# Queries, keys and gates of the first layer with channels on the partitions

## The chip, the cores and the metric

The kernel runs on one core of a Trainium2 chip. The metric is the device time of one execution in microseconds; several executions of a kernel are timed, and the median is compared. One further execution is recorded by the hardware profiler, and the profile shown here is that execution.

The engines are named as in the profile: PE is the matrix engine (PEld its weight loads), DVE the vector engine, ACT the scalar engine, POOL the GpSimd engine, SP the queue that issues most DMAs. Matrix results land in PSUM, which has eight banks of 512 fp32 numbers on each of 128 partitions; everything else that is on the core lies in SBUF.

## The reference, cut to what matters

A backbone of two layers over 1024 latent tokens and 256 context tokens of width 1024, in fp32. Layer 0 mixes by windowed attention with 16 query heads and 4 key heads of 64 channels, layer 1 by latent attention. What the change touches is the projection of layer 0:

```python
def project(h):
    n = h.shape[1]
    q, k, v, g = jnp.split(h @ w_in, [A_WIDTH, A_WIDTH + A_KV_WIDTH, A_WIDTH + 2 * A_KV_WIDTH], axis=-1)
    ...
qx, kx, vx, gx = project(hx)      # latent
qc, kc, vc, gc = project(hc)      # context
qx = apply_rope(qx, cos, sin)
kx = apply_rope(kx, cos, sin)

def apply_rope(u, cos, sin):
    r1, r2, c1, c2 = jnp.split(u, 4, axis=-1)
    rot = jnp.concatenate([-r2, r1, -c2, c1], axis=-1)
    return u * cos + rot * sin
```

`w_in` has 2560 columns: 1024 for queries, 256 keys, 256 values, 1024 gates. `h` is the normalized, scaled and shifted input (adaLN); scale, shift and the output gates come from products of a conditioning vector with the 1024 x 3072 matrix `ada_w` of each layer. Only latent tokens are rotated. In a head of 64 channels the rotation pairs channel i with i + 16 inside each half of 32.

## The kernel before

**Precision.** A product of fp32 matrices is made of three: each operand is split into a high part (`hi`, a rounded copy by ACT) and a low part (`lo`, the difference, by DVE or POOL) in `split`, L118 to L121, and `mm3`, L123 to L127, adds hi x hi, lo x hi and hi x lo in PSUM. So each step over 128 input channels is three matmuls, and 1024 input channels are 24.

**Staging.** SBUF is two large arenas, addressed in KB per partition: `R` for matmul operands, `F` for the rest. The input lies in five tiles `hT[p]` of 256 tokens, channels on the partitions (p = 0 is the context, 1 to 4 are latent, tile p at 16 p KB of `R`). The columns of `w_in` are taken in ten blocks of 256 in the order of `blocks`, L341: values first (block 0), queries (1 to 4), two of gates (5, 6), keys (7), two of gates (8, 9). `fetch` (L344) and `load_w` (L296) load a block's weights in four quarters through a ring of four staging buffers `stg` and split them, low parts on POOL, into one of two places `wst`, so that block n + 1 is fetched when block n begins.

**One block of projection.** For each block and each tile p, `proj_mm` (L373) issues 2 x 24 matmuls in two halves j. For values, queries and keys the input is the stationary operand and the weights move (256 columns): tokens come out on the partitions. For gates it is the other way round: channels come out on the partitions, 256 tokens move. Results go to one of six PSUM banks in turn (`pss`, L115). `proj_out` (L390) takes them out: gates through ACT's Silu to DRAM (`g0_d`); values by a split into `V`; queries and keys of latent tokens by `rope` (L304): DVE multiplies with the cosines (L307), makes the two rotated halves times the sines (L312, twice), POOL adds (L317); the context is copied by DVE (L411). Since attention wants channels on the partitions, `rest` (L416) then transposes each rotated 128 x 128 piece on PE (L421, four for a tile, into banks 6 and 7) and splits the result, into `kT` for keys, and for queries through a ring `qst` to DRAM (`q0_d`) by four DMAs. The loop at L693 calls `rest` of a tile after the matmuls of the next one.

**Beside it.** The loop also advances a generator `ada_vec` (L355) that forms the remaining adaLN products: DVE multiplies a row block of `ada_w` by a scalar and adds it up (L192, L194; called adaLN steps below), the sum is split (low part on POOL) and summed over partitions by four small PE products (L209, two for the last of layer 1, which take a bank of `pss` too). `wo_load` (L610) loads and splits the sixteen halves of the output weights of layer 0 into `Wo`, which lies over `hT`; two are advanced per tile near the end of the projections and what is left when the second attention unit begins. `UnitA` (L475) is one attention unit (128 query tokens, one key head): `prep_q` loads its queries back from `q0_d`, `score` makes scores (L517, L518, L524 to L527), and so on. Layer 1 follows.

**What sets the order.** The program is written for five in-order queues; a scheduler of the framework places each engine's instructions from the program's order and their data, and may move them against each other. Each queue then runs in order and waits on semaphores.

## Time and profile before

| | us |
|---|---|
| median of 3 runs | 1670.13 (1668.36 to 1673.35) |
| profiled execution | 1673.18, span 1671.0, mean granted clock 0.993 |
| projections of layer 0, blocks 1 to 9 | 95 to 386 |
| attention of layer 0 | 386 to 780 |
| layer 1 | 780 to 1671 |

The stages were read off the timeline: the first query block's matmuls begin at 95 us, the last gate's Silu starts at 385.9 us. A row of a group has line, engine, operation, out<-in and shapes, then busy time and mean ns of one, then the idle time of the engine before it and what ended that. A row of windows has the window, its length, and the busy time and count of PE, PEld, DVE, ACT and POOL, then the granted PE clock, the DMA share and GB/s. A row of waits has who waited for whom: us in total, times, longest. A row of the timeline has start and length in us, engine, line, shape and count. Matmuls are pipelined: a matmul's length overlaps the next one's, so the spacing of starts is what PE pays.

### The profile page before, as it was taken

The numbers are of one execution on the slowest core, as the hardware profiler recorded it, in microseconds if no ns is written. First come the engines' busy times: TensorE is split into PE (matmuls) and PEld (weight loads), VectorE is DVE, ScalarE is ACT, GpSimd is POOL, SyncE is SP. The second block draws the span as 40 slices with busy tenths as digits, with TensorE's granted clock in tenths as the row PEclk, the third lists the DMA queues.
The fourth block names the chain that finished last, engine by engine and source line by source line (L and its number), as shares of the span: only waits on it lengthen the run. The fifth ranks groups of instructions, "written<-read, shape, count | busy, mean of one in ns | idle before, by whom it ended". The sixth has DMA issues, their size and how long they took to land.

```text
span 1671.0 us, 27005 instructions
## 1 busy us (share of the span) xinstructions
PE 1613.4 (97%) x9688; PEld 1304.9 (78%) x9688; DVE 975.4 (58%) x2066; ACT 833.5 (50%) x1790; POOL 783.3 (47%) x784
## 2 busy tenths in 40 slices
...
GB/s 304 146 173 207 177 214 84 74 145 128 113 105 89 93 89 92 89 93 201 27 64 243 222 71 74 95 54 20 60 32 38 49 20 53 39 84 69 46 156 65
DMA packets 128070, 175.38 MB, mean 105 GB/s; under 512 B 11184, under 2 KB 75312, under 8 KB 127936
## 3 DMA queue, kind: packets, MB, share of 16 engines
...
HBM read 127.47 MB, written 46.15 MB: 104 GB/s over the span
## 4 chain that ended last, share of the span: by engine, by line
PE 76%; DVE 11%; ACT 5%; issue 4%; DMA 2%; POOL 1%; SPq 0%; DVEq 0%; ACTq 0%; POOLq 0%
PE PB L125 16%; PE PB L127 16%; PE PB L126 16%; PE PB L1125 9%; PE PB L1091 4%; PE PB L555 3%; PE PB L545 3%; DVE arena_r L121 2%; DVE arena_f L194 2%; PE PB L517 2%; DVE arena_f L524 2%; PE PB L518 2%; DVE arena_f L275 1%; ACT arena_f L1110 1%; ACT arena_f L527 1%
## 5 line engine op out<-in xcount | busy, mean ns | idle before, releaser
L125 PE MATMUL PB<-arena_r 128*128 128x256 f32 (+3 forms) x2104 | 691.1, 329 | 5.2 <-ACT arena_r L278 4.1
L126 PE MATMUL PB<-arena_r 128*128 128x256 f32 (+3 forms) x2104 | 681.6, 324 | 2.8 <-DVE arena_r L280 1.5
L127 PE MATMUL PB<-arena_r 128*128 128x256 f32 (+3 forms) x2104 | 678.9, 324 | 0.7 <-DVE arena_r L121 0.7
L125 PEld LDWEIGHTS PB<-arena_r 128*128 128x128 f32 (+1 forms) x2104 | 403.0, 192 | 68.8 <-issue 26.1
L127 PEld LDWEIGHTS PB<-arena_r 128*128 128x128 f32 (+1 forms) x2104 | 402.8, 192 | 31.0 <-DVE arena_r L121 1.3
L126 PEld LDWEIGHTS PB<-arena_r 128*128 128x128 f32 (+1 forms) x2104 | 403.9, 192 | 28.1 <-DVE arena_r L280 3.2
L1117 POOL TENSOR_TENSOR arena_f<-arena_f 128x512 f32<-128x512 f32 x252 | 326.2, 1295 | 76.0 <-ACT arena_f L1110 60.9
L121 DVE TENSOR_TENSOR arena_r<-PB,arena_r 128x512 fp32r<-128x512 f32 (+5 forms) x263 | 168.1, 646 | 143.1 <-ACT arena_r L120 141.4
L1110 ACT ACTIVATE arena_f<-PB 128x512 f32<-128x512 f32 x320 | 189.2, 598 | 124.8 <-PE PB L127 111.8
L1095 DVE TENSOR_REDUCE arena_f<-PB 128x1 f32<-128x1280 f32 x128 | 190.5, 1488 | 97.4 <-PE PB L1091 95.0
L121 POOL TENSOR_TENSOR arena_r<-arena_f,arena_r 128x512 fp32r<-128x512 f32 x98 | 139.1, 1438 | 182.2 <-ACT arena_r L120 140.1
L120 ACT CAST arena_r<-PB 128x512 fp32r<-128x512 f32 (+5 forms) x263 | 142.5, 550 | 91.2 <-PE PB L545 25.1
L524 DVE CUSTOM_DVE_ANT_0 arena_f<-PB,arena_f,small 128x256 f32<-128x256 f32 (+1 forms) x288 | 146.2, 523 | 29.4 <-PE PB L518 23.2
L1125 PE MATMUL PB<-arena_f 128*64 128x512 f32 x640 | 156.0, 599 | 0.0
L527 ACT ACTIVATE arena_f<-arena_f,small 128x640 f32<-128x640 f32 (+2 forms) x160 | 119.4, 747 | 31.1 <-DVE small L526 30.4
L555 PE MATMUL PB<-arena_r 128*128 128x512 f32 x336 | 123.8, 441 | 3.3 <-ACT arena_f L566 2.1
L120 ACT CAST arena_r<-arena_f 128x512 fp32r<-128x512 f32 (+1 forms) x138 | 82.7, 609 | 87.4 <-PE PB L126 18.9
L194 DVE SCALAR_TENSOR_TENSOR arena_f<-arena_f,small 128x512 f32<-128x512 f32 x126 | 108.2, 910 | 7.8 <-DMA arena_f<-ada_w 7.4
L545 PE MATMUL PB<-ident,arena_f 128*128 128x128 f32 x672 | 110.1, 274 | 1.0 <-ACT arena_f L527 0.9
L1125 PEld LDWEIGHTS PB<-arena_f 128*64 128x64 f32 x640 | 43.3, 136 | 80.5 <-issue 79.3
L1091 PE MATMUL PB<-arena_r 96*128 96x512 f32 (+1 forms) x384 | 100.1, 369 | 1.2 <-DVE arena_f L1095 1.0
L545 PEld LDWEIGHTS PB<-ident,arena_f 128*128 128x128 f32 x672 | 83.3, 140 | 19.3 <-ACT arena_f L527 4.6
...
## 6 DMA issues: line engine op xcount, KB each, us to landing
arena_f<-ada_w SPq DMA_DIRECT2D x82, 256.0 KB, 3.4
arena_r<-q_d SPq DMA_DIRECT2D x80, 256.0 KB, 4.0
arena_f<-a_w_in SPq DMA_DIRECT2D x40, 256.0 KB, 3.4
q_d<-arena_f SPq DMA_DIRECT2D x80, 128.0 KB, 2.4
g_d<-arena_f SPq DMA_DIRECT2D x36, 256.0 KB, 3.1
...
arena_r<-qn_d SPq DMA_DIRECT2D x32, 256.0 KB, 3.6
```

The source lines that it names most:

```text
L120: nc.scalar.copy(hi, src)
L121: (lo_eng or nc.vector).tensor_sub(lo, src, hi.bitcast(F32))
L125: nc.tensor.matmul(o, ah, bh, start=first, stop=False)
L126: nc.tensor.matmul(o, al, bh, start=False, stop=False)
L127: nc.tensor.matmul(o, ah, bl, start=False, stop=last)
L524: nc.vector.tensor_tensor_reduce(o, S, mk, 1.0, prev, ALU.add, ALU.max, mx)
L545: nc.tensor.transpose(pt[:, h, :], self.Ps[h][:, ci * 128 : ci * 128 + 128], ident)
L555: nc.tensor.matmul(self.pv, V[:, self.chunks[ci], self.g, :], PT[:, s], start=ci == 0 and s == 0, stop=ci == self.m - 1 and s == 1,)
L1095: nc.vector.reduce_max(self.mx[:, 96 + b : 97 + b], psm[:, 0:TOK], AX.X, negate=True)
L1110: nc.scalar.activation(E, S, AF.Exp)
L1117: eng.tensor_add(self.acc, self.acc, E)
L1125: nc.tensor.matmul(self.pv[p : p + 64], Vq[:, c, self.h % 4, :], self.E.pop(c), start=c < 2, stop=c >= NT - 2)
```

## The change

For blocks 1 to 9 the weights become the stationary operand everywhere, so queries, keys and gates come out with channels on the partitions and nothing is transposed. `proj_t` replaces the old `proj_out` for them. The latent tokens are taken in two groups `gp` = 1, 2 of 512 (two neighbouring tiles seen as one moving operand in two pieces of 256, `hw`) and, for each, two channel halves `c` of 128: 24 matmuls of 512 each. The context (`gp` = 0) keeps 256 moving, 2 x 24 matmuls. Values (block 0) stay as they were.

The rotation of a group: DVE multiplies the bank with the cosines, a DVE shuffle exchanges channels i and i + 16 within each 32 partitions out of PSUM, POOL multiplies the shuffled copy with the (signed) sines and adds. The tables are now 128 channels x 1024 tokens each. `rest` splits queries from SBUF and stores them with four DMAs; for keys DVE adds the rotated halves itself, 64 partitions at a time.

Moved with it: the tables' place takes one of the four staging buffers of `stg`; blocks 8 and 9 run over latent group 1, latent group 2 and the context last, so that the tiles of `hT` come free in another order, and with them the places of `Wo` and of the first two query buffers `qtb`; two output-weight halves are advanced in each of the last six calls that are not of group 1, and two each at attention units 1 and 2.

```diff
@@ -321,9 +321,9 @@
     wst = [80, 96]
     kT = r_at(112, 4, TOK)
     V = r_at(132, NT, 4, 128)
-    cosa = f_at(0, 8, 64)
-    sina = f_at(2, 8, 64)
-    stg = Ring(F, [4, 6, 8, 10], 512)
+    cosa = f_at(0, SEQ)
+    sina = f_at(10, SEQ)
+    stg = Ring(F, [4, 6, 8], 512)
     xr = Ring(F, [14, 18, 48], 1024)
     xtr = Ring(F, [22, 30], 2048)
     ev = Ring(F, [38, 40, 42, 44, 46], 512)
@@ -371,73 +371,101 @@
     ada_steps = ada_vec()
     def proj_mm(bi, p, j, o, ka, kb):
+
         h, W, js = hT[p], wt[bi], slice(j * 128, j * 128 + 128)
         for k in range(ka, kb):
-            hk = [h[:, s, k, :] for s in range(2)]
-            wk = [W[:, s, k, :] for s in range(2)]
-            if blocks[bi] >= 1536:
-                mm3(o, [w[:, js] for w in wk], hk, k == 0, k == 7)
-            else:
-                mm3(o, [x[:, js] for x in hk], wk, k == 0, k == 7)
+            mm3(o, [h[:, s, k, js] for s in range(2)], [W[:, s, k, :] for s in range(2)], k == 0, k == 7)
     def proj_a(bi, p):
-        ps = PB[:, 4, :] if (bi, p) == (9, 4) else pss()
+        ps = pss()
         os = [ps[:, j * 256 : j * 256 + 256] for j in range(2)]
         for j in range(2):
             proj_mm(bi, p, j, os[j], 0, 8)
-        return proj_out(bi, p, os, ps)
...
-    def proj_out(bi, p, os, ps=None):
...
+        proj_out(bi, p, os)
+
+    def proj_out(bi, p, os):
+        for j in range(2):
+            ti = 2 * p + j
+            split(V[:, ti, :, 0:64], V[:, ti, :, 64:128], shp(os[j], 4, 64))
+
+
+    hw = [None]
+    for p in (1, 3):
+        two = R[:, 16 * p * KB : 16 * (p + 2) * KB]
+        hw.append(two.rearrange("p (q s k n) -> p q s k n", q=2, s=2, k=8))
+    swap = [(i + 16) % 32 for i in range(32)]
+
+    def proj_t(bi, gp, c):
+        W, c0 = wt[bi], blocks[bi]
+        ps = PB[:, 4, :] if (bi, gp) == (9, 0) else pss()
+        for cc in (c,) if gp else range(2):
+            if gp:
+                o = shp(ps, 2, 256)
+            elif c0 < 1024:
+                o = shp(ps, 2, 2, 128)[:, :, cc, :]
+            else:
+                o = ps[:, cc * 256 : cc * 256 + 256]
+            for k in range(8):
+                if gp:
+                    m = [hw[gp][:, :, s, k, :] for s in range(2)]
+                elif c0 < 1024:
+                    m = [shp(hT[0][:, s, k, :], 2, 128) for s in range(2)]
+                else:
+                    m = [hT[0][:, s, k, :] for s in range(2)]
+                mm3(o, [W[:, s, k, cc * 128 : cc * 128 + 128] for s in range(2)], m, k == 0, k == 7)
+        t0 = 256 + 512 * (gp - 1) if gp else 0
         if c0 >= 1536:
             g = ev.next()
             nc.scalar.activation(g, ps, AF.Silu)
             ch = (c0 - 1536) // 128
...
+            if gp:
+                load(out=g0_d[ch + c, :, t0 : t0 + 512], in_=g)
+            else:
+                load(out=g0_d[ch : ch + 2, :, 0:256].rearrange("c p n -> p c n"), in_=shp(g, 2, 256))
             return None
...
+        if gp == 0:
+            if c0 == 1024:
+                u = shp(ps, 2, 256)
+                for e in range(2):
+                    kh = kT[:, e::2, 0:256]
+                    split(kh[0:64], kh[64:128], u[64 * e : 64 * e + 64])
             else:
...
+                q = shp(qst.next(), 2, 512)
+                split(q[:, 0].bitcast(F32R), q[:, 1].bitcast(F32R), ps)
                 for e in range(2):
                     for s in range(2):
                         load(
...
+                            out=q0_d[c0 // 256, :, s, 0:2, e * 256 : e * 256 + 256],
+                            in_=shp(q[64 * e : 64 * e + 64, s], 2, 256),
                         )
...
+            return None
+        x0 = t0 - 256
+        a, r = ev.next(), ev.next()
+        nc.vector.tensor_mul(a, ps, cosa[:, x0 : x0 + 512])
+        nc.vector.stream_shuffle(out=r, in_=ps, mask=swap)
+        nc.gpsimd.tensor_mul(r, r, sina[:, x0 : x0 + 512])
+        if c0 < 1024:
+            nc.gpsimd.tensor_add(a, a, r)
+
+        def rest():
+            q = shp(qst.next(), 2, 512)
+            if c0 == 1024:
+                for e in range(2):
+                    es = slice(64 * e, 64 * e + 64)
+                    nc.vector.tensor_add(q[0:64, e], a[es], r[es])
+                    kh = kT[:, 2 * c + e, t0 : t0 + 512]
+                    split(kh[0:64], kh[64:128], q[0:64, e])
+                return
+            split(q[:, 0].bitcast(F32R), q[:, 1].bitcast(F32R), a)
+            for e in range(2):
+                for s in range(2):
+                    o0 = e * 256 + c * 128
+                    load(
+                        out=q0_d[c0 // 256, :, s, t0 // 128 : t0 // 128 + 4, o0 : o0 + 128],
+                        in_=shp(q[64 * e : 64 * e + 64, s], 4, 128),
+                    )
+
+        return rest
     mask = f_at(0, 384)
@@ -451,9 +479,9 @@
     Pr = Ring(F, [14 + 2.5 * i for i in range(8)], 640)
     gr = Ring(F, [1.5, 2.5, 46], 256)
     xr0 = Ring(F, [4], 1024)
-    Wo = [r_at(o, 2, 1024) for o in (0, 8, 16, 24, 32, 40, 48, 56)]
+    Wo = [r_at(o, 2, 1024) for o in (16, 24, 32, 40, 48, 56, 0, 8)]
     ogr = Ring(R, [64, 72], 2048)
-    qtb = [r_at(o, 2, 4, 128) for o in (56, 60, 80, 84, 108)]
+    qtb = [r_at(o, 2, 4, 128) for o in (72, 76, 80, 84, 108)]
     ptr = Ring(R, [88, 92, 96, 100, 104], 1024)
     pss3 = Banks(0, 1, 2)
     pst3 = Banks(6, 7, 3)
@@ -623,8 +651,8 @@
                 yield
 
     wo_fill = wo_load()
-    order = [(0, p) for p in range(2, NP)] + [(bi, p) for bi in range(1, 8) for p in range(NP)]
-    order += [(8, 0), (8, 1), (9, 0), (9, 1), (8, 2), (9, 2), (8, 3), (9, 3), (8, 4), (9, 4)]
+    order = [(bi, gp, c) for bi in range(1, 8) for gp in range(3) for c in range(2 if gp else 1)]
+    order += [(bi, gp, c) for gp in (1, 2, 0) for bi in (8, 9) for c in range(2 if gp else 1)]
     rest = None
     N1, N2 = 3, 7
 
@@ -690,36 +718,39 @@
     xts = {2: shp(xtr.next(), 8, 256)}
     turn_x(nx[4], xts[2], 0)
     turn_x(norm_x(src0(5), xr_0, junk), xts[2], 1)
-    for i, (bi, p) in enumerate(order):
-        if p == (3 if bi == 0 else 0) and bi + 1 < 10:
-            if bi == 0:
-                load(out=cosa, in_=t["cos_a"].rearrange("p (t d) -> p t d", t=8))
-                load(out=sina, in_=t["sin_a"].rearrange("p (t d) -> p t d", t=8))
+    for p in range(2, NP):
+        if p + 1 < NP:
+            xts[p + 1] = build_x(p + 1, src0, xr, xtr, junk)
+        build_h(p, xts.pop(p), hT[p], ada0.A, ada0.B)
+        if p == 3:
+            fetch(1)
+        proj_a(0, p)
+    load(out=cosa, in_=t["cos_a"])
+    load(out=sina, in_=t["sin_a"])
+    started = {0, 1}
+    for bi, gp, c in order:
+        if bi + 1 < 10 and bi + 1 not in started:
+            started.add(bi + 1)
             fetch(bi + 1)
-        if bi == 0:
-            if p + 1 < NP:
-                xts[p + 1] = build_x(p + 1, src0, xr, xtr, junk)
-            build_h(p, xts.pop(p), hT[p], ada0.A, ada0.B, fast=p == 0)
-        else:
-            steps(ada_steps, N1 if bi < 5 else N2 if bi < 7 else 100)
-        if (bi, p) == (9, 2):
+        steps(ada_steps, N1 if bi < 5 else N2 if bi < 7 else 100)
+        if (bi, gp, c) == (9, 2, 0):
             load2(out=mask, in_=t["mask"])
             load2(out=gx, in_=gate_d[0, 0, :].partition_broadcast(128))
             load2(out=gc, in_=gate_d[0, 1, :].partition_broadcast(128))
-        if (bi, p) == (8, 4):
+        if (bi, gp) == (8, 0):
             units[0].prep_q()
             units[0].prep()
             units[1].prep_q()
-        if (bi, p) == (9, 4):
+        if (bi, gp) == (9, 0):
             units[1].prep()
             units[2].prep_q()
             for h in range(4):
                 units[0].score(h)
-        r = proj_a(bi, p)
+        r = proj_t(bi, gp, c)
         if rest:
             rest()
         rest = r
-        if i > 40:
+        if bi >= 8 and gp != 1:
             for _ in range(2):
                 next(wo_fill, None)
 
@@ -738,9 +769,9 @@
     og = None
     fins = []
     for ui, u in enumerate(units):
-        if ui == 1:
-            for _ in wo_fill:
-                pass
+        if ui in (1, 2):
+            next(wo_fill, None)
+            next(wo_fill, None)
         if u.g == 0:
             og = shp(ogr.next(), 2, 8, 128)
             steps = 4 * u.m - 2
@@ -1415,8 +1446,8 @@
         "b_kv_norm": g("b_kv_norm")[0],
         "b_w_ukv": ukv,
         "b_w_out": g("b_w_out")[0],
-        "cos_a": tab(cos_a),
-        "sin_a": tab(sin_a),
+        "cos_a": np.tile(cos_a.T, (2, 1)),
+        "sin_a": np.tile(sin_a.T, (2, 1)),
         "cos_b": tab(cos_b),
         "sin_b": tab(sin_b),
         "mask": mask,
```

37 lines of the change are left out of this document (removed).

## The prediction

> **What bounds the kernel now.** I read four views: the page's head, the windows of the first layer's projection stage, who PE waited for there, and the timelines of PE, DVE and POOL in it. "L" numbers are the kernel's before.
>
> ```profile
> span 1671.0 us, 27005 instructions
> PE 1613.4 (97%) x9688; PEld 1304.9 (78%) x9688; DVE 975.4 (58%) x2066; ACT 833.5 (50%) x1790; POOL 783.3 (47%) x784
> ```
>
> ```profile
> core 0: us, PE busy (x) PEld busy (x) DVE busy (x) ACT busy (x) POOL busy (x), PEclk, DMA share, GB/s
> 95.00:130.00 35.00, 31.30 (x245) 30.36 (x243) 35.00 (x57) 7.69 (x13) 16.59 (x15) 0.95 0.70 199
> 130.00:165.00 35.00, 31.36 (x246) 30.49 (x245) 34.31 (x62) 6.39 (x11) 15.06 (x15) 0.95 0.71 209
> 165.00:201.00 36.00, 34.66 (x286) 33.70 (x284) 27.37 (x51) 6.38 (x11) 16.97 (x15) 1.00 0.65 179
> 201.00:230.00 29.00, 27.30 (x225) 26.35 (x224) 17.61 (x48) 6.09 (x11) 9.20 (x11) 1.00 0.60 162
> ```
>
> ```profile
> PE PB L421 <- POOL arena_f L317: 8.7, 8, 3.4
> PE PB L421 <- DVE arena_f L411: 1.7, 1, 1.7
> ```
>
> The four windows are query blocks 1 to 4. PE is the bound of the kernel. In blocks 1 and 2 it is not: DVE is full (35.00 of 35, 34.31 of 35), the granted clock is 0.95, and a block takes 35 us, while block 4, with less for DVE, takes 29. The link is the transposes, L421: PE's queue holds them behind the next group of matmuls, and they wait for the rotation of the group before (10.4 us in 90 to 386 us). So PE can run one group ahead of DVE and no more.
>
> **PE's own work.** Start times, to the hundredth:
>
> ```profile
> 215.48 0.28 PE L127 MATMUL PB<-arena_r 128*128 128x256 f32 x1
> 215.60 0.60 PE L421 MATMUL PB<-ident,arena_f 128*128 128x128 f32 x4
> 215.96 0.36 PE L125 MATMUL PB<-arena_r 128*128 128x256 f32 x1
> 216.16 0.28 PE L126 MATMUL PB<-arena_r 128*128 128x256 f32 x1
> 216.28 0.29 PE L127 MATMUL PB<-arena_r 128*128 128x256 f32 x1
> ...
> 889.98 0.39 PE L127 MATMUL PB<-arena_r 128*128 128x512 f32 x1
> 890.21 0.39 PE L125 MATMUL PB<-arena_r 128*128 128x512 f32 x1
> ...
> 891.34 0.39 PE L127 MATMUL PB<-arena_r 128*128 128x512 f32 x1
> ```
>
> ```profile
> L209 PE MATMUL PB<-arena_r 128*2 128x512 f32 x28 | 7.7, 403 | 0.0
> L517 PE MATMUL PB<-arena_r 128*128 128x256 f32 x12 | 3.7, 317 | 0.0
> ```
>
> A 256-wide matmul starts 0.12 us after the last (216.16, 216.28). A 512-wide one takes 0.227: from 889.98 to 891.34 are six steps, 1.36 us. Four transposes cost 0.44: without them the matmuls of 215.96 and 216.16 would stand at 215.60 and 215.72.
>
> - Blocks 1 to 9 issue 9 x 240 = 2160 matmuls of 256. After: 9 x 48 = 432 of 256 (context) and 9 x 96 = 864 of 512 (latent). Each of the 864 replaces two: 0.240 - 0.227 = 0.013, so -11.2 us.
> - The 100 transposes, 25 groups of four, go: 25 x 0.44 = -11.0 us.
> - From 95 to 386 us, 291 us, PE's work is 2160 x 0.12 + 11.0 = 270, the adaLN products (L209, 28 of 512 wide, 6.4), the first attention scores (L517 and as many L518, 24 of 256, 2.9) and small transposes (about 1): 280.5. The other 10.5 us are waits and the clock's dips, as the 10.4 above says. With the transposes gone, PE waits for nothing but free banks and weights: up to -10.5.
>
> Most that can be had: 11.2 + 11.0 + 10.5 = 33 us. The rule of back-to-back matmuls in the Trainium skill (TensorE: Matmul & The Clock Gate, section Back-to-back issue gap: N over 2.4, plus 2.5 ns, warm) speaks against the first term: 109 ns for 256 and 216 for 512, so 2.6 ns a pair, an estimate of 2.2 us in place of 11.2. Rows of this kernel have 120 and 227, and the sum goes by them.
>
> **DVE and POOL, which take the work over.** Rows from 84 to 229 us (last rotation of block 4), DVE busy 124.30 us; then rows for the new operations:
>
> ```profile
> 84.00:229.00 145.00, 134.62 (x1079) 131.08 (x1079) 124.30 (x222) 29.05 (x52) 64.68 (x57) 0.98 0.64 182
> ...
> L194 DVE SCALAR_TENSOR_TENSOR arena_f<-arena_f,small 128x512 f32<-128x512 f32 x84 | 77.6, 981 | 4.2 <-DMA arena_f<-ada_w 4.2
> L312 DVE TENSOR_TENSOR arena_f<-PB,arena_f 128x128 f32<-128x128 f32 x62 | 14.8, 280 | 0.0
> L307 DVE TENSOR_TENSOR arena_f<-PB,arena_f 128x256 f32<-128x256 f32 x32 | 13.3, 415 | 15.0 <-PE PB L127 15.0
> L121 DVE TENSOR_TENSOR arena_f<-PB,arena_f 128x512 fp32r<-128x512 f32 x18 | 12.2, 680 | 0.0
> L411 DVE COPY arena_f<-PB 128x256 f32<-128x256 f32 x8 | 3.0, 410 | 0.0
> ...
> L121 POOL TENSOR_TENSOR arena_r<-arena_f,arena_r 128x512 fp32r<-128x512 f32 x26 | 41.3, 1613 | 13.1 <-ACT arena_r L120 6.5 <-PE PB L126 3.7 <-PE PB L127 2.9
> L317 POOL TENSOR_TENSOR arena_f<-arena_f 128x256 f32<-128x256 f32 x30 | 22.4, 750 | 67.0 <-DVE arena_f L312 51.2 <-PE PB L209 13.6 <-PE PB L126 2.1
> ```
>
> ```profile
> L121 DVE TENSOR_TENSOR arena_r<-arena_f,arena_r 128x512 fp32r<-128x512 f32 x32 | 28.8, 910 | 44.6 <-ACT arena_r L120 29.2 <-PE PB L126 15.4
> L604 POOL TENSOR_TENSOR arena_f<-arena_f 128x512 f32<-128x512 f32 x18 | 23.2, 1288 | 58.6 <-DVE arena_f L603 35.1 <-DVE small L526 19.7 <-DVE small L538 3.8
> L120 ACT CAST arena_r<-arena_f 128x512 fp32r<-128x512 f32 x130 | 79.5, 620 | 84.6 <-PE PB L126 18.9 <-DMA arena_f<-a_w_out 13.3 <-PE PB L127 12.3
> ```
>
> Per latent group of a query block (16 of them), after: one product with the cosines out of PSUM (0.68, as the 680 row), one shuffle, one subtraction of the high part, now SBUF from SBUF (0.91). No row has a shuffle. It reads 128x512 f32 out of PSUM and writes SBUF as the 680 row does, and has one operand less: I take 0.68; the ends are the 0.41 of half its size and 1.49, the dearest DVE read of PSUM here (1280 wide). The Trainium skill (VectorE: DVE Perf Modes, section The perf-mode tier table) gives about 2400 ns for 2048 elements; a quarter is an estimate of 0.6, which would change DVE's sum by 1.3 us and the path by nothing.
>
> ```profile
> L1095 DVE TENSOR_REDUCE arena_f<-PB 128x1 f32<-128x1280 f32 x128 | 190.5, 1488 | 97.4 <-PE PB L1091 95.0
> ```
>
> - Removed from DVE: 14.8 + 13.3 + 12.2 + 3.0 = 43.3 us. Added: 16 x (0.68 + 0.68 + 0.91) + 4 x 0.68 (context) = 39.0.
> - POOL: 32 adds of 0.75 become 32 operations (a product with the sines, an add) of 1.29: 24 becomes 41 us, POOL 64.7 becomes 82 of 145. Not a bound. But POOL's long operations hold DVE's adaLN steps up:
>
> ```profile
> 88.46 8.88 DVE L194 SCALAR_TENSOR_TENSOR arena_f<-arena_f,small 128x512 f32<-128x512 f32 x7
> 103.62 4.05 DVE L194 SCALAR_TENSOR_TENSOR arena_f<-arena_f,small 128x512 f32<-128x512 f32 x6
> ...
> 88.55 6.91 POOL L121 TENSOR_TENSOR arena_r<-arena_f,arena_r 128x512 fp32r<-128x512 f32 x4 [2.95 <-PE PB L127]
> ```
>
> Six steps alone take 4.05 us; seven beside four POOL subtractions take 8.88, so each subtraction costs DVE about 1 us. Over the stage: 84 x (0.981 - 0.74) = 20 us for 26 subtractions, 0.78 each. For 32 new long operations: 25 us, between 0 (where DVE works out of PSUM, as beside L317 now) and 33.
>
> Sum for DVE: 124.3 - 43.3 + 39.0 + 25 = 145 us, so DVE ends block 4 at about 229 as now (204 to 237; with a shuffle of 1.49, 13 us more). PE, free, ends it at 95 + 4 x (48 x 0.12 + 96 x 0.227) + 3 = 208. The lag of 21 us decides: results stay in PSUM, and with six banks in turn PE may be five groups ahead, 5 x 24 x 0.227 = 27 us, about 25 with the banks of the adaLN products. So I cost DVE's lateness at 4 us of the 33. Beyond 25 every us is paid in full: at the dear shuffle the lag is 34 and 9 more are lost.
>
> **The rest, by queue.** SP's waits for staging buffers, two transfers' time to landing, and two windows:
>
> ```profile
> SPq L301 <- POOL arena_r L121: 24.9, 20, 5.0
> ...
> q_d<-arena_f SPq DMA_DIRECT2D x80, 128.0 KB, 2.4
> arena_r<-q_d SPq DMA_DIRECT2D x80, 256.0 KB, 4.0
> ...
> 354.00:386.00 32.00, 31.97 (x263) 31.38 (x262) 9.99 (x33) 13.91 (x26) 3.89 (x3) 1.00 0.63 184
> 390.00:420.00 30.00, 28.85 (x172) 22.79 (x172) 26.64 (x108) 28.10 (x80) 11.45 (x18) 1.00 0.40 107
> ```
>
> - Weights of block n+2 are cast while block n+1 runs, a block (28 us) ahead, on ACT behind query casts and on POOL behind rotations: hidden while the lag is under 28. With three staging buffers the fourth quarter's load waits on SP for POOL's subtraction of the first; adaLN loads and query stores queue behind it. SP waits there now too (24.9 us in 20 waits, the longest 5.0), and the quarter has the same block of time. Cost 0; 2 us as upper end.
> - Query stores: 64 of 128 KB in runs of 512 bytes in place of 1 KB. They are 8.4 of the stage's 26.4 MB (145 us at 182 GB/s); were they to take twice as long, the DMA share would go from 0.64 to 0.84. 0.
> - Tables: two loads of 512 KB in place of 256, behind block 0, used 6 us into block 1: at most 2 us, I take 1.
> - Key block: per group product, shuffle, two half adds, two half subtractions, six DVE operations of 0.7 = 4.2 us against PE's 5.45. 0.
> - Output weights: four halves instead of two are left for attention (ui 1 and 2): two more loads, casts on ACT (0.62 each) and subtractions. ACT is nearly full there (28.10 of 30), so +1.2 us.
> - The last blocks run latent first, context last; the query buffers lie in the last latent tile instead of the one before and fill (4.0 us a load), as now, beside two groups (11.5 us). From the first attention units on all queues keep their order. 0.
>
> Sum: 33 - 4 (DVE) - 1 (tables) - 1.2 (attention) - 2 (what PE still waits at block ends) = 25 us. The profiled execution took 1673.18 us, 3.05 over the median of the runs, 1670.13: 1648 against its own time, 1645 as a median.
>
> **Rivals.**
> - PE stays tied to DVE (through weights behind query casts on ACT and POOL): blocks 1 to 4 still end at 229. After it only 5 x (28.8 - 27.55) and five key transposes at 0.44 are won: 8.4 - 1.2 = 7, 1663. For: DVE's sum does not fall. Against: no PE instruction of the stage reads a rotated query any more.
> - Pairing wins 2.2 instead of 11.2 us, if a moving operand in two pieces of 256, which no row has, costs 10 ns more than one of 512: 864 x 0.0104 = 9, 1654. Against: 0.227 in one piece and 0.12 for half. The Trainium skill's rule of back-to-back matmuls, above, would end here too.
> - Slower: DVE stands still in each rotation. Its subtraction waits in order for POOL's two operations and ACT's cast, 1.29 + 1.29 + 0.62 = 3.2 us. If nothing is queued between, 16 x 3.2 = 51 us: 51 - 25 (banks) - 7 = +19, 1689. It decides from 16 x d > 37, d over 2.3 us a group; a shuffle of 3 us would do the same. Against: adaLN steps are queued between shuffle and subtraction in most groups, three of them at up to 1.78.
> - The stage gets shorter and attention starts no earlier, held by query loads: about 1669. Against: their 4.0 us, and ACT and DVE under half busy in 354 to 386.
>
> **Numbers.** Forecast (gain 18 to 34): 0.60. Tied: 0.18. Pairing: 0.07. Slower: 0.11. No change: 0.04. 1645 is the first; its own range is 1636 to 1652. 1636 to 1664 adds the tied and the pairing cases and leaves 0.15 out. Faster by over 0.3% (5 us, about what a measurement here can tell): the first three, 0.85, less 0.02 for a tied case that gains nothing: 0.83; same 0.06; slower 0.11.
>
> **What would show it.** Right: blocks 1 to 4 at 28 us each, clock 1.00; no PE wait on POOL; matmuls of 512 every 0.227; shuffle 0.6 to 0.7; DVE full to about 230 and PE a block ahead; projections done near 360 in place of 386, and the same 1285 us behind. Wrong: PE idle before first matmuls of groups, released by DVE's shuffle, or DVE idle before the subtraction on ACT's cast.

## The result, and the profile after

The changed kernel takes 1680.9 us (median of 4 runs, 1680.5 to 1681.6) against 1669.2 us for the kernel before on the same chip: a ratio of 1.0062, 95% interval 1.0047 to 1.0076. It is slower by about 10 us, where 25 us less were predicted. The profiled execution's span is 1678.9 us. "L" numbers are now those of the changed kernel: L125 to L127 the block matmuls, L444 the cosine product, L445 the shuffle, L446 and L448 POOL's sine product and add, L120 and L121 cast and subtraction, L194 the adaLN steps, L220 and L226 in `AdaLN.cols` ACT's copy of an adaLN column block and the four small transposes that read it, L419 the gates, L463 the query stores.

The page's head:

```profile
span 1678.9 us, 24936 instructions
PE 1594.1 (95%) x8724; PEld 1247.4 (74%) x8724; DVE 996.2 (59%) x2004; ACT 831.6 (50%) x1790; POOL 808.4 (48%) x780
```

PE's busy time fell by 19 us, and the span grew by 8. All of that lies in the projection stage. The last gate of block 9 starts at 395.4 us where it was 385.9, and what follows takes 1283.5 us, 1285.1 before. In every run below it takes 1283.4 to 1285.1. So the start of the last gate measures a version of the kernel.

The windows over blocks 1 to 5 (columns as in the prediction):

```profile
95.00:130.00 35.00, 35.00 (x179) 29.50 (x178) 34.59 (x39) 6.37 (x11) 21.91 (x15) 1.00 0.55 157
130.00:165.00 35.00, 33.77 (x172) 28.17 (x170) 27.87 (x37) 4.63 (x8) 17.66 (x12) 1.00 0.61 165
165.00:201.00 36.00, 24.35 (x120) 20.32 (x120) 28.84 (x35) 5.57 (x10) 17.84 (x12) 0.84 0.61 170
201.00:230.00 29.00, 15.64 (x59) 11.93 (x59) 19.54 (x27) 4.01 (x7) 16.48 (x10) 0.74 0.55 154
230.00:251.00 21.00, 4.45 (x22) 4.43 (x23) 15.48 (x21) 4.93 (x9) 15.59 (x11) 0.50 0.62 174
251.00:306.00 55.00, 55.00 (x281) 45.62 (x280) 15.63 (x20) 13.37 (x23) 15.56 (x13) 1.00 0.44 136
```

PE is full up to 165 us, as predicted, and again from 251 on. Between them it waits for a large part of the time, at a granted clock down to 0.50. From 251 to the last gate it needs 144 us for four blocks of gates, the keys and the first scores, near the prediction's rate (five blocks at 27.55 us are 138, and the scores). What PE waited for, and the long wait in its timeline:

```profile
PE PB L226 <- ACT arena_f L220: 27.1, 1, 27.1
PE PB L125 <- DVE arena_f L445: 13.4, 3, 8.8
PE PB L125 <- DVE arena_f L121: 2.3, 1, 2.3
```

```profile
246.55 0.58 PE L226 MATMUL PB<-ident,arena_f 2*128 2x2 f32 x4 [27.05 <-ACT arena_f L220]
...
247.66 0.41 PE L125 MATMUL PB<-arena_r 128*128 128x256 f32 x1
247.88 0.41 PE L126 MATMUL PB<-arena_r 128*128 128x256 f32 x1
...
251.22 0.28 PE L127 MATMUL PB<-arena_r 128*128 128x256 f32 x1
251.34 0.28 PE L125 MATMUL PB<-arena_r 128*128 128x256 f32 x1
```

Four waits are for banks, three that the shuffle frees (13.4 us) and one that the context's subtraction frees (2.3). The longest is none of a query's: PE came to the small transposes of layer 1's first adaLN column at 219.5 us, in the first group of block 5, and stood there for 27 us. After it a 256-wide matmul starts every 0.21 us instead of 0.12, until 251. The transposes read a copy on ACT, and ACT's queue says why that copy was late. First its groups from 84 to 251 us (after the bar: idle before them, and for what), then its timeline:

```profile
L120 ACT CAST arena_f<-arena_f 128x512 fp32r<-128x512 f32 x15 | 9.3, 620 | 112.6 <-POOL arena_f L448 94.6 <-DMA q_d<-arena_f 18.0
```

```profile
234.58 0.62 ACT L120 CAST arena_f<-arena_f 128x512 fp32r<-128x512 f32 x1 [10.87 <-POOL arena_f L448]
...
243.17 0.62 ACT L120 CAST arena_f<-arena_f 128x512 fp32r<-128x512 f32 x1 [6.93 <-POOL arena_f L448]
...
245.93 0.57 ACT L220 COPY arena_f<-PB 2x512 f32<-2x512 f32 x1
```

Fifteen query casts wait for POOL's add, and the copy stands in order behind them. The rotation's lateness so reaches PE through an instruction that has nothing to do with queries. Why the rotation itself is late shows in the window from the first shuffle (103.8 us) to the last of block 4 (245.4 us), and in DVE's groups in it:

```profile
103.80:245.44 141.64, 99.96 (x489) 82.63 (x487) 114.32 (x140) 22.68 (x41) 79.95 (x51) 0.85 0.58 160
```

```profile
L194 DVE SCALAR_TENSOR_TENSOR arena_f<-arena_f,small 128x512 f32<-128x512 f32 x66 | 76.8, 1210 | 13.1 <-DMA arena_f<-ada_w 13.1
L121 DVE TENSOR_TENSOR arena_f<-arena_f 128x512 fp32r<-128x512 f32 x15 | 12.9, 859 | 7.4 <-ACT arena_f L120 6.2
L445 DVE STREAM_SHUFFLE arena_f<-PB 128x512 f32<-128x512 f32 x15 | 10.9, 729 | 0.0
L444 DVE TENSOR_TENSOR arena_f<-PB,arena_f 128x512 f32<-128x512 f32 x16 | 10.9, 680 | 0.0
L192 DVE TENSOR_SCALAR arena_f<-arena_f,small 128x512 f32<-128x512 f32 x8 | 5.6, 744 | 6.8 <-DMA arena_f<-ada_w 6.8
```

An adaLN step takes 1.21 us in the mean (0.98 before; busy time counts the small overlap of neighbouring steps once, so it is less than count times mean). One by one the steps are of two kinds: 36 of the 66 take 0.73 to 0.75 us, the other 30 take 1.74 to 1.83, and none lies between. Two stretches of three steps, and what POOL ran from 109 to 117 us:

```profile
109.30 2.07 DVE L194 SCALAR_TENSOR_TENSOR arena_f<-arena_f,small 128x512 f32<-128x512 f32 x3
...
112.52 4.14 DVE L194 SCALAR_TENSOR_TENSOR arena_f<-arena_f,small 128x512 f32<-128x512 f32 x3
```

```profile
112.70 1.70 POOL L446 TENSOR_TENSOR arena_f<-arena_f 128x512 f32<-128x512 f32 x1 [4.71 <-DVE arena_f L445]
114.49 1.62 POOL L448 TENSOR_TENSOR arena_f<-arena_f 128x512 f32<-128x512 f32 x1
```

Every step of the long kind lies beside a POOL operation. So POOL does not slow a step a little: it leaves it alone or costs it about 1 us. DVE is also idle for 141.6 - 114.3 = 27.3 us, of which 19.9 are waits for adaLN loads and 6.2 for ACT's casts. The prediction had DVE full.

### The profile page after: what moved, and what is told of

Read it like the earlier page. It is cut to its first block, busy times and chain, and to the rows that moved or that the text cites. A ratio compares the mean times of both kernels' runs of the same rounds, so it can differ in the third digit from the quotient of the medians.

```text
span 1678.9 us, 24936 instructions
## 1 busy us (share of the span) xinstructions
PE 1594.1 (95%) x8724; PEld 1247.4 (74%) x8724; DVE 996.2 (59%) x2004; ACT 831.6 (50%) x1790; POOL 808.4 (48%) x780
## 4 chain that ended last, share of the span: by engine, by line
PE 72%; DVE 11%; ACT 6%; issue 5%; POOL 4%; DMA 2%; SPq 0%; DVEq 0%; POOLq 0%; ACTq 0%
PE PB L125 15%; PE PB L127 15%; PE PB L126 15%; PE PB L1156 9%; PE PB L1122 4%; PE PB L583 3%; PE PB L573 3%; DVE arena_r L121 2%; DVE arena_f L194 2%; PE PB L545 2%; DVE arena_f L552 1%; POOL arena_f L446 1%; PE PB L546 1%; DMA arena_f<-ada_w 1%; DVE arena_f L275 1%
## 5 line engine op out<-in xcount | busy, mean ns | idle before, releaser
L125 PE MATMUL PB<-arena_r 128*128 128x512 f32 (+3 forms) x1816 | 639.5, 353 | 20.3 <-DVE arena_f L445 13.4
L126 PE MATMUL PB<-arena_r 128*128 128x512 f32 (+3 forms) x1816 | 630.7, 348 | 3.6 <-DVE arena_r L280 2.6
L127 PE MATMUL PB<-arena_r 128*128 128x512 f32 (+3 forms) x1816 | 627.8, 347 | 0.6 <-DVE arena_r L121 0.6
L125 PEld LDWEIGHTS PB<-arena_r 128*128 128x128 f32 (+1 forms) x1816 | 346.2, 191 | 97.3 <-issue 26.0
L127 PEld LDWEIGHTS PB<-arena_r 128*128 128x128 f32 (+1 forms) x1816 | 345.5, 191 | 42.5 <-DVE arena_r L121 1.2
L126 PEld LDWEIGHTS PB<-arena_r 128*128 128x128 f32 (+1 forms) x1816 | 346.7, 191 | 40.5 <-DVE arena_r L280 4.5
L121 DVE TENSOR_TENSOR arena_r<-PB,arena_r 128x512 fp32r<-128x512 f32 (+4 forms) x255 | 162.5, 644 | 139.7 <-ACT arena_r L120 138.2
L121 POOL TENSOR_TENSOR arena_r<-arena_f,arena_r 128x512 fp32r<-128x512 f32 x98 | 139.4, 1437 | 182.9 <-ACT arena_r L120 139.8
L120 ACT CAST arena_r<-PB 128x512 fp32r<-128x512 f32 (+4 forms) x255 | 137.8, 549 | 68.7 <-PE PB L573 29.7
L194 DVE SCALAR_TENSOR_TENSOR arena_f<-arena_f,small 128x512 f32<-128x512 f32 x126 | 125.8, 1042 | 22.2 <-DMA arena_f<-ada_w 22.0
L555 ACT ACTIVATE arena_f<-arena_f,small 128x640 f32<-128x640 f32 (+2 forms) x160 | 119.4, 747 | 28.4 <-DVE small L554 27.1
L120 ACT CAST arena_r<-arena_f 128x512 fp32r<-128x512 f32 (+2 forms) x146 | 86.7, 609 | 86.6 <-DVE arena_f L455 18.6
```

Of the source, the lines that this page charges most:

```text
L120: nc.scalar.copy(hi, src)
L121: (lo_eng or nc.vector).tensor_sub(lo, src, hi.bitcast(F32))
L125: nc.tensor.matmul(o, ah, bh, start=first, stop=False)
L126: nc.tensor.matmul(o, al, bh, start=False, stop=False)
L127: nc.tensor.matmul(o, ah, bl, start=False, stop=last)
```

## The experiments

Each is the changed kernel with the edit shown, unless said otherwise. "Ratio" is to the kernel before on the same chip; shuffle and gate are the starts, in us, of the last shuffle of block 4 and of the last gate, in the profiled execution. The runs were timed on several chips, on which the kernel before took 1669.2 to 1672.1 us, so ratios compare better than differences in us, which are good to 2 or 3. Nor does the stage begin at the same time in all: the first shuffle lies between 102.5 and 109.3 us (103.8 in the changed kernel).

| run | median us | ratio (95%) | shuffle | gate |
|---|---|---|---|---|
| changed kernel | 1680.9 | 1.0062 (1.0047 to 1.0076) | 245.4 | 395.4 |
| a1_fewer_steps | 1680.0 | 1.0044 (1.0031 to 1.0058) | 237.4 | 395.8 |
| a2_turn_later | 1674.7 | 1.0015 (1.0004 to 1.0026) | 247.2 | 388.3 |
| a3_stores_later | 1684.5 | 1.0070 (1.0048 to 1.0091) | 249.6 | 401.0 |
| a4_no_pool | 1649.1 | 0.9860 (0.9845 to 0.9875) | 214.8 | 364.6 |
| b1_aside | 1673.9 | 1.0017 (1.0007 to 1.0026) | 235.4 | 386.7 |
| b2_sub_pool | 1690.5 | 1.0117 (1.0097 to 1.0137) | 246.0 | 404.9 |
| b3_ahead | 1682.3 | 1.0077 (1.0054 to 1.0100) | 243.7 | 393.6 |
| b4_dve_rot | 1651.9 | 0.9886 (0.9870 to 0.9902) | 215.7 | 365.3 |
| d2_half | 1670.0 | 0.9996 (0.9984 to 1.0009) | 236.8 | 382.5 |
| c4_before_dve | 1664.7 | 0.9968 (0.9958 to 0.9977) | none | 378.7 |
| c1_both | 1649.6 | 0.9876 (0.9855 to 0.9897) | 221.0 | 364.6 |
| c2_stores_pool | 1653.4 | 0.9896 (0.9876 to 0.9915) | 227.3 | 365.5 |
| c3_256 | 1664.5 | 0.9964 (0.9951 to 0.9977) | 226.8 | 379.9 |
| d1_two_later | 1652.6 | 0.9887 (0.9868 to 0.9907) | 216.8 | 365.5 |
| e1_weights_pool | 1643.2 | 0.9837 (0.9819 to 0.9855) | 226.7 | 360.2 |
| e2_weights_pool_only | 1659.7 | 0.9936 (0.9921 to 0.9951) | 222.9 | 374.3 |

### Is it the long wait, VectorE, SP or POOL?

**The small transposes moved.**

```
 mt = pst()[:, 0:8] ...   # the four transposes and the add behind them
+now only for layer 1's first column: kept, and issued at (bi, gp, c) == (6, 0, 0)
```

> The changed kernel, with the four small transposes of layer 1's first adaLN column (and VectorE's add behind them) issued ahead of block 6 in place of in block 5's first group. Nothing else moves. Theory 'one in-order wait': PE's 27.1 us wait there is itself the loss, since three banks are free for gates of block 5 while VectorE finishes block 4: the wait is gone, PE waits for banks under 8 us more, 1652 to 1660 us. Rival 'VectorE sets it': the wait only shows VectorE's lateness and goes over to full banks or to block 6's weights, whose casts stand on ACT behind the same query casts: over 18 us of PE's idle time are found there, 1672 to 1681.

6 us won (8 by the ratios), where the wait was 27. PE's waits:

```profile
PE PB L125 <- DVE arena_f L454: 22.3, 5, 8.5
PE PB L235 <- ACT arena_f L220: 6.0, 3, 5.2
```

(L454 is the shuffle there, L235 the transposes.) With the wait gone PE runs into full banks for 22.3 us. The wait was VectorE's lateness in another coat, and the rival holds.

**Fewer adaLN steps beside the queries.**

```
-    N1, N2 = 3, 7
+    N1, N2, N7 = 2, 8, 8     # N7: per group of block 7
```

> The changed kernel, with two adaLN steps a group in the query blocks in place of three, eight in blocks 5 and 6 in place of seven, eight in each group of the key block in place of all that are left in its first. Theory 'VectorE sets it': 20 steps of about 0.8 to 1.2 us leave the query blocks, so the last shuffle of block 4, at 245.4 us in the changed kernel, comes 16 to 24 us earlier (221 to 229); PE's waits for banks (13.4 us) and the 27.1 us wait of the small transposes fall to under 10 together; 1645 to 1655 us. Rival 'SP feeds it too slowly' (adaLN loads queued behind query stores): VectorE still stands still once a block, the last shuffle comes under 10 us earlier, 1670 to 1680. Both get slower again if blocks 5 to 7 become bound by the steps moved there: PE waits in 251 to 360, which the changed kernel has not.

The last shuffle comes 8 us earlier and the time stays. By these numbers it is the rival's case, at its edge, but not by its cause. The framework's scheduler, which places the queues, still put the same six steps or so into a rotation in blocks 1 and 2, and where they then ran out, in block 4, DVE stood for ACT's cast instead: its waits for it, from 84 to 251 us, went from 6.2 to 17.6 us. The stage also began 4 us later here (first shuffle 107.7 us), which hides a part of what was won. (Steps that run in the key block write their split parts where the keys lie, so this kernel spoils part of the keys.)

**Stores later, loads earlier.**

```
-            for e in range(2): ... load(out=q0_d[...], in_=...)
+            return store            # issued one group later
```

> The changed kernel, with the four stores of a query group issued one group later, so that SP's queue does not wait for that group's casts and subtractions before it issues the next adaLN loads. Theory 'SP feeds it too slowly': VectorE's idle time for ada_w loads (13.1 and 6.8 us in 84 to 251) falls under 5 us, the last shuffle comes 12 to 18 us earlier (227 to 233), and as the small transposes wait for what follows it, the time falls by about as much: 1663 to 1669 us. Rival 'SP is no cause' (the loads themselves, or the fourth weight quarter held by three staging buffers, keep VectorE waiting): the idle time stays over 12 us and the time within 4 us of the changed kernel's 1681.

```
-                w = stage.next()
-                load(out=w, in_=t["ada_w"][...])
+                w = stage.next()    # loaded two loads earlier
```

> The changed kernel, with each adaLN load issued two loads ahead of the step that reads it, so that SP has it out before it comes to the query stores that wait for casts. 'SP's order': VectorE's idle time for ada_w (20 us in 84 to 251) falls under 6 us, the last shuffle comes 10 to 16 us earlier, and the 27 us wait of the small transposes shrinks by as much: 1665 to 1672 us. Rival 'the idle time only stands where VectorE would wait for the rotation anyway': it turns into waits for ACT's cast, the last shuffle comes under 5 us earlier, 1677 to 1683.

Neither moved the time clear of its interval, and neither tested its theory, though the times are those of the rivals. The edits changed the program's order, and the scheduler put SP's queue back: in both runs loads and stores alternate as in the changed kernel. SP's timeline of the changed kernel, then of b3_ahead (where L481 and L169 are stores and adaLN loads):

```profile
146.80 3.73 SPq L463 DMA_DIRECT2D q_d<-arena_f  x4
150.63 3.45 SPq L189 DMA_DIRECT2D arena_f<-ada_w  x3
157.25 2.58 SPq L463 DMA_DIRECT2D q_d<-arena_f  x4
```

```profile
145.76 3.48 SPq L481 DMA_DIRECT2D q_d<-arena_f  x4
149.34 2.71 SPq L169 DMA_DIRECT2D arena_f<-ada_w  x3
155.22 2.57 SPq L481 DMA_DIRECT2D q_d<-arena_f  x4
```

**Without POOL's half of the rotation.**

```
-        nc.gpsimd.tensor_mul(r, r, sina[...])
-        if c0 < 1024:
-            nc.gpsimd.tensor_add(a, a, r)
+        if c0 >= 1024:
+            nc.gpsimd.tensor_mul(r, r, sina[...])
```

> The changed kernel without POOL's two operations of each query rotation (the product with the sines and the add): it leaves out that part of the rotation of the queries, while VectorE still issues product, shuffle and subtraction. Theory 'POOL's long operations hold VectorE's adaLN steps up': these steps take a mean of 0.95 us or less in place of 1.17, 84 x 0.2 = 17 us less, the query casts no longer wait for POOL's add, and the last shuffle comes 17 to 30 us earlier; 1650 to 1660 us. Rival 'the steps' cost is VectorE's own or of the other POOL work (the weights' subtractions)': their mean stays over 1.1, the last shuffle comes less than 10 us earlier, 1672 to 1681.

32 us less than the changed kernel, and DVE's own instructions between first and last shuffle are the same (140 in both), so the two can be subtracted (window, then a group of DVE, from its first to its last shuffle):

```profile
107.58:214.75 107.17, 94.95 (x491) 80.20 (x489) 93.17 (x140) 22.00 (x39) 33.05 (x19) 0.96 0.74 208
```

```profile
L194 DVE SCALAR_TENSOR_TENSOR arena_f<-arena_f,small 128x512 f32<-128x512 f32 x66 | 56.7, 905 | 11.0 <-DMA arena_f<-ada_w 11.0
```

141.6 - 107.2 = 34.4 us; 114.3 - 93.2 = 21.1 of it is busy time, 20.1 in the 66 steps (76.8 - 56.7), and the other 13.3 is idle time (27.3 against 14.0). So POOL's 30 operations in this stretch cost DVE about 0.7 us each by slowing its steps, and 13 us by making it wait: the 6.2 for casts, and 6 of the 19.9 for adaLN loads.

### Slowed steps, or the chain over POOL?

**POOL works, nobody waits for it.**

```
-            nc.gpsimd.tensor_add(a, a, r)
+            nc.gpsimd.tensor_add(r, r, sina[...])
```

> The changed kernel, where POOL does both of its operations of a query rotation, but the second adds into r, which nobody reads: casts and subtractions take the cosine product alone, so the sine half of the rotation is missing from the queries. POOL's work and its meeting with VectorE stay; nobody waits for it. Rival readings of the 31 us that the kernel without these operations won. 'Contention' (POOL's long operations slow VectorE's steps): the steps stay at a mean of 1.1 us or more, the last shuffle of block 4 stays after 238 us (245.4 in the changed kernel), 1668 us or more. 'Chain' (shuffle, POOL twice, cast, subtraction in order, with product and shuffle of the next group behind them): the last shuffle comes before 228, 1648 to 1658 us, whatever the steps' mean.

The same window and groups:

```profile
102.70:235.41 132.71, 101.02 (x491) 83.74 (x489) 114.85 (x142) 21.89 (x39) 81.48 (x47) 0.89 0.61 168
```

```profile
L194 DVE SCALAR_TENSOR_TENSOR arena_f<-arena_f,small 128x512 f32<-128x512 f32 x66 | 68.7, 1086 | 11.3 <-DMA arena_f<-ada_w 11.3
L121 DVE TENSOR_TENSOR arena_f<-arena_f 128x512 fp32r<-128x512 f32 x15 | 20.7, 1383 | 4.2 <-ACT arena_f L120 4.2
```

DVE's busy time stays where it was (114.9 us); steps a little shorter, subtractions longer, as most of them now fall beside POOL's operations. Only idle time shrinks, from 27.3 to 17.9 us. Between the two cases, nearer to contention: of the 32 us, 7 (by the time) to 9 (by the idle time) are the chain's.

**The subtraction on POOL.**

```
-            split(q[:, 0]..., q[:, 1]..., a)
+            split(q[:, 0]..., q[:, 1]..., a, nc.gpsimd)
```

> The changed kernel, with the subtraction that gives the queries' low parts on POOL in place of VectorE, so that nothing in VectorE's queue waits for a rotation; ACT's casts still do. VectorE loses 16 operations of 0.86 us (14 us) and 6 us of waits, POOL gets 16 of 1.3 to 1.7 (21 to 27 us) that may hold VectorE's steps up. 'Chain' (VectorE's place in it costs the time): the last shuffle comes 15 to 20 us earlier, 1660 to 1667 us. 'Contention': the steps' mean rises from 1.17 towards 1.3 (84 x 0.15 = 12 us) and takes the gain back: within 5 us of 1681.

10 us slower than the changed kernel. More work on POOL makes it worse, and its chain longer; the steps' mean stays (1.18 us from 84 to 251, 1.17 in the changed kernel), but waits for adaLN loads rise from 19.9 to 23.9 us. Neither case as put.

**POOL's two operations on VectorE, and one of the two.**

```
-        nc.gpsimd.tensor_mul(r, r, sina[...])
-            nc.gpsimd.tensor_add(a, a, r)
+            nc.vector.tensor_mul(r, r, sina[...])    # d2_half: nc.gpsimd
+            nc.vector.tensor_add(a, a, r)
```

> The changed kernel, with the sine product and the add of the query rotation on VectorE. VectorE gets 32 operations of about 0.85 us (27 us); POOL loses 32 of 1.3 to 1.7. 'Contention': the steps' mean falls from 1.17 to about 0.95 (17 us), so VectorE ends 10 us later or so, 1681 to 1692. 'Chain': rotation from shuffle to cast takes 2.3 us in place of 3.5 to 5, ACT's queue and SP's with it move on earlier, and VectorE's 30 us of idle time pay for the added work: 1660 to 1675.

> The changed kernel, with the query rotation's add alone on VectorE; the sine product stays on POOL. 16 of POOL's 32 operations are left. 'Contention' (each POOL operation costs VectorE's steps alike): half of the 29 us that VectorE's taking both won, 1664 to 1669 us, the steps' mean near 1.0 us (1.17 with both on POOL, 0.85 with none). 'Chain' (what costs is that the rotation goes over to POOL and comes back before the subtraction): with one trip left, most of the loss stays, 1672 or more, or most of it goes when the two POOL operations in a row were the trouble, 1658 or less.

With both on VectorE the kernel is 29 us faster than the changed one and beats the kernel before (0.9886), more than either case as put allowed. The window between first and last shuffle and DVE's groups in it, the two operations in lines L447 and L448:

```profile
103.37:215.66 112.29, 94.95 (x491) 80.19 (x489) 104.02 (x160) 23.66 (x42) 33.24 (x22) 0.94 0.71 191
```

```profile
L194 DVE SCALAR_TENSOR_TENSOR arena_f<-arena_f,small 128x512 f32<-128x512 f32 x57 | 44.1, 795 | 8.1 <-DMA arena_f<-ada_w 8.1
L447 DVE TENSOR_TENSOR arena_f<-arena_f 128x512 f32<-128x512 f32 x15 | 13.5, 899 | 0.1
...
L448 DVE TENSOR_TENSOR arena_f<-arena_f 128x512 f32<-128x512 f32 x15 | 11.8, 789 | 0.1
```

DVE takes on 25.3 us of work and still has less to do, 104.0 against 114.3 us: its steps fall from 1.21 to 0.80 us (57 x 0.41 = 24 us; 3 of the 57 are of the long kind), nine fewer stand in the stretch, and idle time falls from 27.3 to 8.3. With one operation left on POOL, 11 of the 29 us are won, where half (14) would be proportional. DVE's add now waits for POOL's product, which may be what is missing (d2_half, 84 to 251 us):

```profile
L448 DVE TENSOR_TENSOR arena_f<-arena_f 128x512 f32<-128x512 f32 x16 | 17.5, 1094 | 15.2 <-POOL arena_f L447 15.2
```

So both mechanisms are shown, contention the larger (a4_no_pool, b1_aside); how the 29 us divide between them is not shown to the us.

**The kernel before with its add on VectorE** (first layer only).

```
-        nc.gpsimd.tensor_add(o, o, tmp)
+        (eng or nc.gpsimd).tensor_add(o, o, tmp)     # eng = nc.vector in proj_out
```

> The kernel before, with the add that ends each query and key rotation of the first layer (128x256) on VectorE in place of POOL: 40 adds of about 0.45 us more on VectorE (18 us), POOL's 0.75 gone. 'POOL's long operations are what cost the changed kernel its gain': here the adds stand beside VectorE's work out of PSUM and are half as long, so little is won: PE's 8.7 us of waits for POOL's add go, VectorE gets 18 us more in blocks 1 and 2 where it is full; within 6 us of the kernel before. Rival 'any rotation work is better on VectorE': 8 us or more faster, and then a part of what the changed kernel wins with the rotation on VectorE is not the change's own.

5 us faster than the kernel before, within the 6 expected, so a part of the gain is POOL's alone. Like with like, with the queries' rotation on VectorE in both, the change is worth 0.9968 - 0.9886, 0.8% or 13 to 14 us.

### Was PE's sum of 33 us right?

**Rotation on VectorE, and the first column's transposes later** (the edits of b4_dve_rot and a2_turn_later).

> The changed kernel, with the query rotation's sine product and add on VectorE and the four small transposes of layer 1's first adaLN column issued ahead of block 6. With the rotation on VectorE alone PE lost 17.8 us to these transposes and nothing to banks (1651.9 us). Theory 'once VectorE is on time the in-order wait is the whole loss': 1633 to 1638 us, the granted clock 1.00 from 95 to 396. Rival, as in the changed kernel itself, where the wait of 27.1 us went over to banks and 6 us were won: 1646 or more.

**The same, second column's too** (issued at (6, 2, 1)).

> The changed kernel, with the query rotation's sine product and add on VectorE, and the small transposes of both of layer 1's first adaLN columns issued later (the first ahead of block 6, the second ahead of its last group). With the first alone moved, the second one's transposes stood in PE's queue for 9.6 us at 227 us, behind a copy on ACT behind a cast that waits for a VectorE step. 'In-order waits of these transposes are what is left': no PE wait over 4 us from 95 to 396, the last gate at 350 to 355 us in place of 364.6, 1636 to 1641 us, which is the prediction's sum of 33 us with next to nothing lost. Rival 'VectorE's lateness comes back as full banks': 1646 or more, with PE waits for the shuffle of over 8 us.

The rotation on VectorE alone leaves one wait of PE, 17.8 us at the small transposes, none for banks. Moving them wins 2 us or nothing, where 11 to 19 were expected (c1_both's stage began 4 us later than the other two's, so it may have won more there): the wait went to the second column's transposes (9.6 us, c1_both), then to the third's. PE's waits in d1_two_later, and ACT's timeline there:

```profile
PE PB L235 <- ACT arena_f L220: 13.0, 1, 13.0
PE PB L125 <- DVE arena_f L454: 2.8, 1, 2.8
```

```profile
254.42 0.62 ACT L120 CAST arena_r<-arena_f 128x512 fp32r<-128x512 f32 x1 [18.01 <-DMA arena_f<-a_w_in]
...
256.42 0.57 ACT L220 COPY arena_f<-PB 2x512 f32<-2x512 f32 x1
```

Now ACT's queue stood behind a cast of block weights, whose load stood in SP's queue behind adaLN loads that wait for VectorE's steps.

**That load on another queue.** Block weights 2 to 9 are loaded from POOL's queue, where the buffer's release is POOL's own work; with the transposes of both columns later, and without.

```
-    load_w(wt[bi], w_in, stg, 8, 256, ...)
+    load_w(wt[bi], w_in, stg, 8, 256, ..., load=nc.gpsimd.dma_start if bi > 1 else load)
```

> The changed kernel, with the query rotation on VectorE, the small transposes of both columns later (as in d1_two_later), and the loads of block weights 2 to 9 on POOL's queue in place of SP's, where they stood behind adaLN loads that wait for VectorE's steps: in d1_two_later ACT waited 18 us for one quarter of block 6's weights, and the copy for the next small transposes stood behind that cast, PE behind the copy (13.0 us). 'It is the order in SP's queue, handed on through ACT to PE': that wait falls under 4 us, the last gate comes at 350 to 356 us (365.5), 1637 to 1643 us. Rival 'the adaLN steps themselves are late, whatever the queues': PE waits 8 us or more for the same copies, within 4 us of d1_two_later.

> The same without moving the small transposes: rotation on VectorE, weights' loads on POOL's queue. The 17.8 us wait at the first transposes is behind query casts, which wait for VectorE and not for weights: it stays over 12 us, and the time within 4 us of the 1651.9 us of the rotation on VectorE alone. Were it to fall under 8 us and the time to 1645 or less, the weights' place in SP's queue would have been behind that wait too.

e1_weights_pool is the fastest of all, 1643.2 us, ratio 0.9837, at the upper end of what was expected, its last gate 4 us later than that. Its PE waits:

```profile
PE PB L125 <- DVE arena_f L454: 6.8, 1, 6.8
...
PE PB L235 <- ACT arena_f L220: 0.6, 1, 0.6
```

The last gate stands at 360.2 us, 25.7 before that of the kernel before, with 6.8 us still waited for a bank: 32.5 together, against the prediction's 33. That is agreement of the total: it does not measure the three terms apart, and PE's shorter waits and its slower clock after waits are in neither figure. Without moving the transposes the weights' queue made the kernel 8 us slower than b4_dve_rot, where no change was expected (the wait at the transposes grew from 17.8 to 22.4 us): a chain of in-order waits pays only when its last link goes.

**Query stores on POOL's queue** (c1_both with `load` of the stores as `nc.gpsimd.dma_start`).

> The same as c1_both, with the query stores on POOL's queue in place of SP's, which then holds weights and adaLN loads only. 'SP's order feeds VectorE too slowly': VectorE's idle time for ada_w in 84 to 251 (18 us with the rotation on VectorE) falls under 6 us. If VectorE sets anything still, the time falls by 3 to 10 us below c1_both; if PE is the bound, it stays within 3 us of it. Against: POOL's queue holds the weights' subtractions behind stores that wait for VectorE; PE would then wait for weights, above c1_both.

DVE's idle time for adaLN loads falls from 14.9 to 0.6 us (84 to 251), which a3 and b3 could not show: SP's order was its cause. But the last shuffle comes 6 us later, and the time does not fall. DVE's sine product and add in c2_stores_pool (in c1_both their means are 958 and 715 ns), then the timelines of DVE and POOL around one of these products:

```profile
L456 DVE TENSOR_TENSOR arena_f<-arena_f 128x512 f32<-128x512 f32 x16 | 21.4, 1340 | 0.1
L457 DVE TENSOR_TENSOR arena_f<-arena_f 128x512 f32<-128x512 f32 x16 | 16.3, 1017 | 0.1
```

```profile
187.81 5.40 DVE L456 TENSOR_TENSOR arena_f<-arena_f 128x512 f32<-128x512 f32 x1
```

```profile
185.08 2.53 POOL L474 DMA_DIRECT2D q_d<-arena_f  x4 [1.27 <-ACT arena_f L120]
187.62 5.03 POOL L121 TENSOR_TENSOR arena_r<-arena_f,arena_r 128x512 fp32r<-128x512 f32 x4
```

The means are longer by 0.3 to 0.4 us, but issuing the 80 stores, 0.63 us each, is not what costs DVE. Of the 16 products, 14 take 0.67 to 0.69 us, six of them while POOL issues stores; the other two take 5.4 and 6.5 us, each beside four of the weights' subtractions that POOL runs in a row. In c1_both POOL is idle before its subtractions for 104.5 us (84 to 251), almost all for their own casts; here for 15.5, and for 50.7 before the stores, mostly for the queries' casts. So the subtractions stood ready behind stores that waited, and then ran in a row.

**Pairing by itself** (c1_both with each 512-wide matmul as two of 256).

```
-                o = shp(ps, 2, 256);  m = hw[gp][:, :, s, k, :]
+                for q in range(2):  o = shp(ps, 2, 256)[:, q, :];  m = hw[gp][:, q, s, k, :]
```

> The same as c1_both, with each latent matmul of 512 tokens as two of 256, all else alike: 864 more matmuls and weight loads. Prediction's rows (0.120 and 0.227 us from start to start): 864 x 0.013 = 11 us slower than c1_both, less what falls where PE waits. The back-to-back rule of the Trainium skill (TensorE: Matmul & The Clock Gate), 109 and 216 ns: 864 x 0.0026 = 2 us slower.

14.8 us slower than c1_both: the prediction's 11.2 us, since the starts are 0.120 us apart here and 0.227 in c1_both, and 3.6 that fell elsewhere, such as 3.0 us of PE's waits for query loads that c1_both has not. The back-to-back rule of the Trainium skill (TensorE: Matmul & The Clock Gate, Back-to-back issue gap) would have given 2 us; this case's measurement decides against it.

## Why the prediction was wrong

**Right.** Pairing: 11.2 forecast, 14.8 between the runs and 11.2 by the spacing of starts. PE's sum of 33 us: 32.5 in e1_weights_pool, as a total. Shuffle: 0.73 us, taken as 0.68. POOL as no bound: it is busy for 80.0 of the 141.6 us between the shuffles. Its hold-up, 25 us at 0.78 each: 20.1 us in steps, about 0.7 each. DVE's work in block 1 to 4, 145 us: 137.3 us busy from 84 to 251. The part behind the stage: 1283.5 us, unchanged.

**Wrong, first step: "so DVE ends block 4 at about 229 as now (204 to 237; with a shuffle of 1.49, 13 us more)".** That set DVE's time equal to DVE's work. DVE was idle for 27.3 us between its first and last shuffle and ended at 245.4. In the kernel before its idle time of 20.7 us (145 - 124.3) was mostly waiting for PE (15.0 us), and so counted as free. After, other waits took its place. 13 us come from POOL's operations (a4_no_pool): DVE waits for the cast behind them, and SP, whose stores wait for the same casts, brings adaLN loads late. The sentence "Cost 0; 2 us as upper end" for SP's queue was this mistake: 19.9 us of DVE's idle time are waits for adaLN loads behind SP's stores. I had looked at who waits on SP, and not at what stands behind.

**Wrong, second step: "with six banks in turn PE may be five groups ahead, 5 x 24 x 0.227 = 27 us, about 25 with the banks of the adaLN products. So I cost DVE's lateness at 4 us of the 33".** PE's lead has two ends, and I counted one. Its queue also holds layer 1's small transposes, which I entered as "about 1" us of PE's work and not as a wait. They wait for an ACT copy behind query casts, and stopped PE for 27.1 us from 219.5 on. Removing them alone gives 6 us (a2_turn_later), since DVE's lateness then fills the banks. So the first step's error is the larger, and the second decides only once DVE is on time, as b4_dve_rot with its 17.8 us shows. The account of the stage closes, to about 1 us, on these waits: PE's grew from 10.4 to 42.8 us (27.1 + 13.4 + 2.3), 32 more, and the matmul work that was saved, 11.2 and 11.0, takes 22 off; the last gate came 9.5 us later.

**Wrong on the way: "PE, free, ends it at 95 + 4 x (48 x 0.12 + 96 x 0.227) + 3 = 208. The lag of 21 us decides".** The stage begins at 95 us in neither kernel, though the section on the profile before says so. In the changed kernel the context of block 1 is done before this:

```profile
90.31 0.40 PE L125 MATMUL PB<-arena_r 128*128 128x512 f32 x1
```

Block 4's last matmul starts at 214.7 us, 13.4 us of bank waits included, so a free PE would have ended near 201. (In the kernel before, the 96 matmuls of context and first latent tile ahead of the first transposes, at 101.0 us, reach back to about 88, an estimate at 0.12 us each.) With 201 for 208, DVE's own 229 would already have been a lag of 28 us, beyond the 25 that the banks were to cover.

**The rivals.** The rival that ends slower, "DVE stands still in each rotation", had the place nearly right (casts and POOL's two operations hold the queue) and came nearest in time: 1689 against 1680.9. Its price, over 2.3 us of standing a group, is not what happened: 27.3 us over 15 groups are 1.8, and most of them for loads. "PE stays tied to DVE" was right that PE is tied, and wrong in the link: not weights, but banks and an adaLN column. "Pairing wins 2.2" and "attention starts no earlier" fall.

**The check I named** ("PE idle before first matmuls of groups, released by DVE's shuffle, or DVE idle before the subtraction on ACT's cast") shows in the profile: 13.4 and 6.2 us. The larger items, 27.1 and 19.9 us, were not on it.
